# A weight stream in units of four blocks instead of eight, with five buffers for each split part instead of two

## The chip, the core and the metric

The kernel runs on one core of a Trainium2 chip. Its engines are TensorE (PE in the profile, with its weight loads as PEld), VectorE (DVE), ScalarE (ACT), GpSimd (POOL) and SyncE (SP, which issues nearly all the transfers here). The metric is the device time of one execution in microseconds (us); less is better.

## The reference

It is one step of a two-layer diffusion backbone over 128 context and 256 latent tokens, with 1024 features, in float32. Cut to what matters here:

```python
for l in range(2):                                   # per layer, for both streams of tokens
    mod = silu(c) @ w_ada[l] + b_ada[l]              # 9 modulations of 1024 features
    x = LN(alpha*x + 0.5*gate1 * ((silu(a)*g) @ ffn1_w_out))   # a, g = split(mod1(x) @ ffn1_w_in), 2816 wide
    z = mod2(x) @ w_in                               # inputs of the three mixers and of their gates
    o = sig(ga)*(window_attention(z) @ proj_a) + sig(gb)*(neighbourhood_attention(z) @ proj_b) \
        + sig(gc)*(rwkv_scans(z) @ proj_c)
    x = LN(alpha*x + gate2 * (o @ w_out))
    x = LN(alpha*x + 0.5*gate3 * swiglu2(mod3(x)))   # the second feed-forward, as the first
```

## The kernel before

All 384 tokens are one tile of 384 columns, and 128 features lie on the partitions, so a product of a weight block of 128x128 with 128 features of all tokens is one pass of PE with 384 columns. The weights (3344 blocks of 128x128 float32) come as one **stream** in the order of their use. Each block is split into two float32r parts: `hi`, a rounded copy that ACT writes, and `lo`, the rest, which DVE subtracts (`raw - hi`). With the activations split likewise, a block costs three matmuls: `wh xh`, `wh xl` and `wl xh` (`mm3`, lines 381 to 389, and `mm3_steps`, 391 to 401, which hands over two blocks at a time). Only the third one reads `lo`.

The class `Stream` does this in units. `fetch` (line 367) issues one transfer of a unit into a buffer `raw` on SP (line 369), one ACT instruction for `hi` and one or two DVE instructions for `lo`. All three tiles lie in rings: a transfer waits until the `lo` that read its buffer last is done, and an ACT copy waits until PE has used the last block of the unit that lay in its buffer of `hi` before.

Each engine runs its instructions in a fixed queue. A scheduler orders the queues ahead of the run by the program's order and by priorities: `tc.high_priority(offset=...)` around `fetch` lets a unit's instructions go ahead of the work around them by as much as the offset (1500 mostly, 100 beside the scans), as far as a buffer is free, and `tc.issue_after` ties an instruction behind another. Outside the steady state (`stream.steady` false, at the starts of phases) `stream.ahead()` places the units by hand.

The stages of a layer, with the names that the rows use:

- A **feed-forward** (`ffn`): products `pg` and `pa` of the first weight (lines 387 to 389), the gated result `si`, split into `uh` and `ul`, and products `po` of the second weight (lines 397 to 399). Beside the first feed-forward of layer 0, the second, and the first of layer 1, DVE also computes the modulations: `acc <- adaw, cs, acc`, 1024 columns each, whose weights `adaw` come in transfers of their own. In layer 0's first feed-forward the modulations that are needed at once are computed in a startup on PE (`ada`, line 1739).
- A layer norm (`Norm`) that goes with the last products: `ax` takes in `gate * po` chunk by chunk. After the fourth chunk a pilot mean `mu` is subtracted (`ax <- ax,mu`), and the sums go through `stat`, `sv`, `dd` and `rs`.
- A **head** (`Head`): the next phase's first products run already on an input without the norm's scale (`hd`, lines 699 to 701), and the scale is put in afterwards through `wb`, `si` and `sg` (before the mixers through `kx`, `vx`, `qx`).
- **Attention**, two kinds, among dense products `pz`; then the **RWKV scans**, with more dense products (`pz`, `pp`, `pc`) where the scans leave PE free; then the output projection (`po` again).

The names in front of the arrow are written, those behind it read; nearly all DVE, ACT and POOL instructions go through one helper and have its line, 290 (291 after the change).

Of the kernel before, what the change touches and what calls it, by code (L numbers as in the profile page):

```python
# [15 lines left out]
P = 128  # L16
# [13 lines left out]
UNIT = 8  # L30
# [161 lines left out]
# sets of four groups of 256 modulations; the first two are what the first chunks of features need, then the others  # L192
# [3 lines left out]
def _layout(inp):  # L196
    """Rearranges the inputs (permutations and concatenations only)."""
# [36 lines left out]
    # [l][d][h = (p, e)][v][k] -> [l][(e, k)][p][d][v]  # L234
# [8 lines left out]
def _weights(inp, order):  # L243
    """The large weights as 128 x 128 blocks in the order of their use."""
# [22 lines left out]
def _unlayout(r):  # L267
# [7 lines left out]
    st = r["o_st"].reshape(DEPTH, 2, HD, 4, 2, HD)  # l, e, k, p, d, v  # L275
# [4 lines left out]
class Engine:  # L280
    """An engine that knows its last instruction."""
# [14 lines left out]
def trunk(tc, I, O, order, taps=None, stop=None):  # L296
# [5 lines left out]
    def then(*engines):  # L302
        """Behind the last instruction so far of these engines."""
        st = ExitStack()
        for e in engines or (V, S, G):
            if e.last is not None:
                st.enter_context(tc.issue_after(e.last.ins))
        return st
# [32 lines left out]
    class Stream:  # L341
        def __init__(self):
            self.unit = 0
            self.left = []
            self.offset, self.parts, self.steady = 1500, 1, True
# [12 lines left out]
        def ahead(self):  # L358
            """Out of the steady state: the unit after the next is split as soon as the last is used up."""
            if len(self.left) <= UNIT and self.unit < WS_UNITS:  # L360
                self.fetch(self.offset)
# [4 lines left out]
        def fetch(self, offset=0):  # L366
            with tc.high_priority(offset=offset) if offset else ExitStack():
                raw = ring.tile([P, UNIT * P], F32, tag="raw", bufs=3, name="raw")
                nc.sync.dma_start(out=raw, in_=I["ws"][self.unit])
            self.unit += 1  # L370
            hi = ring.tile([P, UNIT * P], F32R, tag="hi", bufs=2, name="hi")
            lo = ring.tile([P, UNIT * P], F32R, tag="lo", bufs=2, name="lo")
            S.activation(out=hi, in_=raw, func=AF.Copy)
            n = UNIT * P // self.parts
            for j in range(0, UNIT * P, n):
                V.tensor_tensor(out=lo[:, j : j + n], in0=raw[:, j : j + n], in1=hi[:, j : j + n].bitcast(F32), op=ALU.subtract)
# [5 lines left out]
    def mm3(out, chunks, xs, after=()):  # L382
        """out += sum of W_k^T x_k, with both factors as sums of two float32r parts."""
# [7 lines left out]
    def mm3_steps(out, chunks, xs, step=2):  # L391
        """mm3 in steps of a few chunks, with what each costs."""
# [10 lines left out]
    def split(dst_h, dst_l, src, lo_eng):  # L403
        """src (SBUF or PSUM, float32) = dst_h + dst_l."""
# [30 lines left out]
    def ada_beside(pool, n):  # L435
        """The next n steps with the products on the vector engine: where that has time, and the tensor engine has not."""
# [38 lines left out]
    def ada_flush():  # L475
        """To columns: out[feature, (block, group, stream)]."""
# [20 lines left out]
    ax = [act.tile([P, NTOK], F32, name=f"ax{c}") for c in range(KD)]  # L497
    # (four more columns: see Norm)
# [8 lines left out]
    class Norm:  # L507
        """Layer norm over the features of y = alpha x + gate * out, chunk by chunk as out comes.
        The next phase's input is h = rs g1 (y - mu) + b1, g1 and b1 per feature and stream, rs and mu per token. Its
        first products W^T h run on z = g1 y, before rs and mu are known: rs W^T z - rs mu W^T g1 + W^T b1, with g1 and  # L510
        b1 as four more columns of z."""
# [1279 lines left out]
```

## Time and profile before

| | us |
|---|---|
| three runs | 2444.65, 2437.09, 2435.69 |
| their median | 2437.09 |
| the profiled execution's span | 2439.6 |

The profiled execution has no time of its own beside its span, which runs from its first to its last instruction; 2439.6 lies 2.5 us above the median of the runs and inside their spread. The stages on the profile's time, in us: startup to 42; layer 0's first feed-forward to 330, head and attention to 580, scans to 870, output projection to 932, second feed-forward to 1240; layer 1's first feed-forward to 1545, attention to 1785, scans to 2072, output projection to 2140, second feed-forward to the end.

How to read it: PE is the engine that is busy nearly all of the time, so the reader looks for the gaps in PE and for what ended each of them. "Waits" lists these by engine and line; a timeline shows what the releasing engine did instead; windows give the busy time of each engine in a stretch and the TensorE clock granted in it (1.00 is the upper level).

### The profile page before, as it was taken

To read this page: it belongs to the slowest core of one execution; us is meant where nothing else is said; L and a number is where in the kernel's file an instruction comes from. 1 tells how busy PE (TensorE), PEld (TensorE's weight loads), DVE (VectorE), ACT (ScalarE), POOL (GpSimd) and SP (SyncE) were. 2 spreads that over 40 slices of the span, in tenths; PEclk is the share of its full clock that TensorE was granted. 3 is DMA by queue.
4 is the path that set the end of the run, shared out by engine and by line. 5 is a ranking of instruction groups with operands and counts; after the bars stand their busy time and mean duration, and the time that the engine had idled before them with its cause. 6 is when DMAs were issued, how large, how long until landed. Compare 5 with 4: busy or idle time off the path is not lost.

```text
span 2439.6 us, 42863 instructions
## 1 busy us (share of the span) xinstructions
PE 2297.4 (94%) x17066; PEld 2106.5 (86%) x17066; DVE 1696.6 (70%) x2865; ACT 1056.4 (43%) x1942; POOL 550.0 (23%) x522
## 2 busy tenths in 40 slices
PE   7999999998899998999999999899989999999998
PEld 5999988897777788999889999889877777889997
DVE  3797886777767568786978954776787674665534
ACT  3333245655545445333243332555555454443332
POOL 2111422101122044211432113310022220542113
PEclk9999999999999999999999999999999999999999
DMA  8575644242111262665546743523321113534332
GB/s 314 193 240 198 191 122 130 84 111 78 40 57 47 72 209 95 191 217 180 180 147 205 244 130 122 154 81 91 112 70 39 51 50 90 204 102 140 130 121 87
DMA packets 125079, 324.54 MB, mean 133 GB/s; under 512 B 31568, under 2 KB 50256, under 8 KB 124880
## 3 DMA queue, kind: packets, MB, share of 16 engines
q1 hardware_dynamic: 124880, 321.81, 41.1%
q8 instruction: 134, 2.20, 0.4%
q14 instruction: 65, 0.53, 0.1%
HBM read 312.06 MB, written 9.70 MB: 132 GB/s over the span
## 4 chain that ended last, share of the span: by engine, by line
PE 71%; DVE 15%; ACT 5%; issue 4%; DMA 3%; POOL 2%; SPq 0%; POOLq 0%; ACTq 0%; DVEq 0%
PE po L399 5%; PE po L398 5%; PE po L397 5%; PE pa L387 4%; PE pg L389 4%; PE pa L388 4%; PE pg L387 4%; PE pg L388 4%; PE pa L389 4%; DVE lo L290 3%; DVE acc L290 2%; PE pz L397 2%; DMA adaw<-wada 2%; ACT hi L290 2%; PE pz L398 2%
## 5 line engine op out<-in xcount | busy, mean ns | idle before, releaser
L290 DVE TENSOR_TENSOR lo<-raw,hi 128x1024 fp32r<-128x1024 f32 (+1 forms) x472 | 583.8, 1246 | 305.9 <-ACT hi L290 303.8
L290 ACT ACTIVATE hi<-raw 128x1024 fp32r<-128x1024 f32 x418 | 441.7, 1058 | 785.0 <-issue 267.5
L290 DVE SCALAR_TENSOR_TENSOR acc<-adaw,cs,acc 128x1024 f32<-128x1024 f32 x224 | 292.3, 1327 | 0.0
L290 POOL TENSOR_TENSOR ul<-si,uh 128x384 fp32r<-128x384 f32 x88 | 126.3, 1435 | 579.3 <-ACT uh L290 579.3
L399 PE MATMUL po<-uh,lo 128*128 128x384 f32 x704 | 238.6, 339 | 6.3 <-DVE lo L290 6.3
L397 PE MATMUL po<-uh,hi 128*128 128x384 f32 x704 | 239.7, 340 | 0.0
L398 PE MATMUL po<-ul,hi 128*128 128x384 f32 x704 | 238.0, 338 | 0.0
L387 PE MATMUL pg<-zh,hi 128*128 128x384 f32 x656 | 224.1, 342 | 9.1 <-DVE si L290 9.1
L388 PE MATMUL pg<-zl,hi 128*128 128x384 f32 x656 | 223.8, 341 | 0.0
L389 PE MATMUL pg<-zh,lo 128*128 128x384 f32 x656 | 223.2, 340 | 0.0
L387 PE MATMUL pa<-zh,hi 128*128 128x384 f32 x632 | 216.2, 342 | 4.9 <-ACT si L290 4.4
L389 PE MATMUL pa<-zh,lo 128*128 128x384 f32 x632 | 213.8, 338 | 0.6 <-DVE lo L290 0.6
L388 PE MATMUL pa<-zl,hi 128*128 128x384 f32 x632 | 214.2, 339 | 0.0
L399 PEld LDWEIGHTS po<-uh,lo 128*128 128x128 f32 x704 | 133.5, 190 | 7.3 <-DVE lo L290 7.3
L397 PE MATMUL pz<-zh,hi 128*128 128x384 f32 x352 | 128.1, 364 | 8.5 <-ACT hi L290 5.7
L397 PEld LDWEIGHTS po<-uh,hi 128*128 128x128 f32 x704 | 133.7, 190 | 2.2 <-issue 0.8
L398 PEld LDWEIGHTS po<-ul,hi 128*128 128x128 f32 x704 | 133.5, 190 | 1.4 <-issue 0.8
L387 PEld LDWEIGHTS pg<-zh,hi 128*128 128x128 f32 x656 | 125.0, 191 | 10.0 <-ACT hi L290 6.7
L399 PE MATMUL pz<-zh,lo 128*128 128x384 f32 x352 | 126.3, 359 | 4.1 <-DVE lo L290 4.0
L387 PEld LDWEIGHTS pa<-zh,hi 128*128 128x128 f32 x632 | 119.1, 188 | 9.8 <-ACT si L290 5.3
L389 PEld LDWEIGHTS pg<-zh,lo 128*128 128x128 f32 x656 | 125.6, 191 | 1.6 <-issue 1.6
L388 PEld LDWEIGHTS pg<-zl,hi 128*128 128x128 f32 x656 | 125.0, 191 | 1.6 <-issue 1.6
(390 smaller groups left out, 5157.4 us busy)
## 6 DMA issues: line engine op xcount, KB each, us to landing
raw<-ws SPq DMA_DIRECT2D x418, 512.0 KB, 3.5
adaw<-wada SPq DMA_DIRECT2D x144, 512.0 KB, 4.8
bm<-rpb SPq DMA_DIRECT2D x64, 64.0 KB, 7.1
axd<-ax SPq DMA_DIRECT2D x16, 192.0 KB, 5.2
gcd<-gt SPq DMA_DIRECT2D x16, 192.0 KB, 4.7
gc<-gcd SPq DMA_DIRECT2D x16, 192.0 KB, 3.4
ax<-axd SPq DMA_DIRECT2D x16, 192.0 KB, 4.8
xt<-xt SPq DMA_DIRECT2D x8, 192.0 KB, 8.6
```

The costliest lines, as they stand in the source:

```text
L290: self.last = f(*a, **k)
L387: T.matmul(out, wh, xh, start=(k == 0), stop=False)
L388: T.matmul(out, wh, xl, start=False, stop=False)
L389: T.matmul(out, wl, xh, start=False, stop=(k == n - 1))
L397: T.matmul(out, wh, xh, start=(k == 0), stop=False)
L398: T.matmul(out, wh, xl, start=False, stop=False)
L399: T.matmul(out, wl, xh, start=False, stop=(k == n - 1))
```

## The change

A unit has 4 blocks (512 columns, 256 KB) instead of 8 (1024 columns, 512 KB). The ring of `raw` has 4 buffers instead of 3, those of `hi` and `lo` 5 instead of 2. In blocks, `raw` goes from 24 to 16 and each part from 16 to 20; the sum stays 56. `lo` is always written by one instruction a unit; before, it took two of 512 columns beside the scans and one of 1024 elsewhere. `ahead()` fetches units while 12 or fewer blocks are left, where it fetched one when 8 or fewer were left. The startup fetches four units ahead in place of two, the same 16 blocks. The rest of the difference is comments and line numbers.

```diff
-UNIT = 8
+UNIT = 4
+RAWS, PARTS = 4, 5
...
-            self.offset, self.parts, self.steady = 1500, 1, True
+            self.offset, self.steady = 1500, True
...
         def ahead(self):
-            if len(self.left) <= UNIT and self.unit < WS_UNITS:
+            while len(self.left) <= (PARTS - 2) * UNIT and self.unit < WS_UNITS:
                 self.fetch(self.offset)
...
         def fetch(self, offset=0):
             with tc.high_priority(offset=offset) if offset else ExitStack():
-                raw = ring.tile([P, UNIT * P], F32, tag="raw", bufs=3, name="raw")
+                raw = ring.tile([P, UNIT * P], F32, tag="raw", bufs=RAWS, name="raw")
                 nc.sync.dma_start(out=raw, in_=I["ws"][self.unit])
             self.unit += 1
-            hi = ring.tile([P, UNIT * P], F32R, tag="hi", bufs=2, name="hi")
-            lo = ring.tile([P, UNIT * P], F32R, tag="lo", bufs=2, name="lo")
+            hi = ring.tile([P, UNIT * P], F32R, tag="hi", bufs=PARTS, name="hi")
+            lo = ring.tile([P, UNIT * P], F32R, tag="lo", bufs=PARTS, name="lo")
             S.activation(out=hi, in_=raw, func=AF.Copy)
-            n = UNIT * P // self.parts
-            for j in range(0, UNIT * P, n):
-                V.tensor_tensor(out=lo[:, j : j + n], in0=raw[:, j : j + n], in1=hi[:, j : j + n].bitcast(F32), op=ALU.subtract)
+            V.tensor_tensor(out=lo, in0=raw, in1=hi.bitcast(F32), op=ALU.subtract)
...
-                stream.offset, stream.parts = 100, 2
+                stream.offset = 100
...
-                    for _ in range((2, 1, 0, 0)[c0 // 2]):
+                    for _ in range((4, 1, 0, 0)[c0 // 2]):
                         stream.fetch()
```

Over the whole queues, DVE has 364 instructions more, ACT 418 more and SP 418 more transfers; PE and POOL have as many as before. Three places of the queues:

The first is DVE in layer 0's first feed-forward, from the subtraction of the pilot mean on; before:

```order
L290 TENSOR_TENSOR ax_83<-ax_83,mu 128x384
L290 SCALAR_TENSOR_TENSOR acc<-adaw,cs,acc 128x1024
L290 TENSOR_TENSOR lo<-raw,hi 128x1024
L290 SCALAR_TENSOR_TENSOR acc<-adaw,cs,acc 128x1024 x3
L290 TENSOR_TENSOR lo<-raw,hi 128x1024
L290 SCALAR_TENSOR_TENSOR acc<-adaw,cs,acc 128x1024 x2
L290 TENSOR_TENSOR lo<-raw,hi 128x1024
L290 SCALAR_TENSOR_TENSOR ax_84<-po,gate,ax_84 128x128
```

and now:

```order
L291 TENSOR_TENSOR ax_83<-ax_83,mu 128x384
L291 SCALAR_TENSOR_TENSOR acc<-adaw,cs,acc 128x1024
L291 TENSOR_TENSOR lo<-raw,hi 128x512
L291 SCALAR_TENSOR_TENSOR acc<-adaw,cs,acc 128x1024
L291 TENSOR_TENSOR lo<-raw,hi 128x512
L291 SCALAR_TENSOR_TENSOR acc<-adaw,cs,acc 128x1024
L291 TENSOR_TENSOR lo<-raw,hi 128x512
L291 SCALAR_TENSOR_TENSOR acc<-adaw,cs,acc 128x1024
L291 TENSOR_TENSOR lo<-raw,hi 128x512
L291 SCALAR_TENSOR_TENSOR acc<-adaw,cs,acc 128x1024 x2
L291 TENSOR_TENSOR lo<-raw,hi 128x512
L291 SCALAR_TENSOR_TENSOR ax_84<-po,gate,ax_84 128x128
```

Two subtractions of 8 blocks stood between groups of one, three and two modulation products; five of 4 blocks stand now one behind each product, so that three products in a row are gone. What stands ahead of this place has also moved: 480 blocks are split there now, where it were 472.

The second is DVE at the start of a feed-forward, where the sums of the layer norm arrive (`sv`); before:

```order
L290 COPY sv<-stat 128x6
L290 TENSOR_TENSOR sv<-sv,stat 128x6
L290 TENSOR_TENSOR dd<-sv 128x3
L290 TENSOR_TENSOR lo<-raw,hi 128x1024
L290 TENSOR_TENSOR dd<-sv,dd 128x3
L290 TENSOR_TENSOR ax_79<-ax_79,mean 128x384
L290 TENSOR_TENSOR ax_80<-ax_80,mean 128x384
L290 RECIPROCAL rs<-dd 128x3
```

and now:

```order
L291 COPY sv<-stat 128x6
L291 SCALAR_TENSOR_TENSOR zl_100<-ax_85,gb,zh_99 128x256
L291 SCALAR_TENSOR_TENSOR zl_102<-ax_86,gb,zh_101 128x128
L291 SCALAR_TENSOR_TENSOR zl_102<-ax_86,gb,zh_101 128x256
L291 TENSOR_TENSOR lo<-raw,hi 128x512 x2
L291 TENSOR_TENSOR sv<-sv,stat 128x6
L291 TENSOR_TENSOR dd<-sv 128x3
L291 TENSOR_TENSOR dd<-sv,dd 128x3
L291 TENSOR_TENSOR ax_79<-ax_79,mean 128x384
L291 TENSOR_TENSOR ax_80<-ax_80,mean 128x384
L291 RECIPROCAL rs<-dd 128x3
```

The subtraction between the two `dd`, 8 blocks, has gone from there, and two of 4 blocks stand ahead of `sv <- sv,stat` instead. From there to the first `si`, DVE has 20 blocks to split where it had 32.

The third is ACT at the start of layer 1's mixers, behind the value input `vx`; before:

```order
L290 ACTIVATE vx<-vx,wb 128x128
L290 ACTIVATE vx<-vx,wb 128x256
L290 ACTIVATE zh_99<-h 128x384
L290 ACTIVATE zh_101<-h 128x384
L290 ACTIVATE hi<-raw 128x1024 x2
L290 ACT_TABLE_LOAD
L290 ACTIVATE ax_81<-pz 128x384
L290 ACTIVATE qx<-qx,wb 128x128
L290 ACTIVATE qx<-qx,wb 128x256
```

and now:

```order
L291 ACTIVATE vx<-vx,wb 128x128
L291 ACTIVATE vx<-vx,wb 128x256
L291 ACTIVATE zh_99<-h 128x384
L291 ACTIVATE zh_101<-h 128x384
L291 ACTIVATE hi<-raw 128x512 x5
L291 ACTIVATE qx<-qx,wb 128x128
L291 ACTIVATE hi<-raw 128x512
L291 ACTIVATE qx<-qx,wb 128x256
L291 ACTIVATE hi<-raw 128x512
L291 ACTIVATE vt<-vt 128x384
L291 ACT_TABLE_LOAD
L291 ACTIVATE ax_79<-ax_79,wb 128x128
```

The query input `qx` stood behind a table load and the copy `ax <- pz`; it now stands ahead of the table load, behind 20 blocks of `hi`, and another 8 blocks stand among its pieces.

## Rows read from the trace of the kernel before

**Rows 1.** The page, section 1: busy time of each engine over the span.

```profile
PE 2297.4 (94%) x17066; PEld 2106.5 (86%) x17066; DVE 1696.6 (70%) x2865; ACT 1056.4 (43%) x1942; POOL 550.0 (23%) x522
```

**Rows 2.** Windows: busy us of PE, PEld, DVE, ACT, POOL; PEclk; DMA share; GB/s.

```profile
50.00:100.00 50.00, 50.00 (x288) 50.00 (x287) 26.54 (x26) 17.57 (x24) 9.55 (x6) 1.00 0.53 175
100.00:150.00 50.00, 48.45 (x294) 45.73 (x293) 48.86 (x45) 16.50 (x24) 6.62 (x5) 1.00 0.77 251
320.00:332.00 12.00, 12.00 (x76) 11.24 (x75) 7.20 (x13) 4.38 (x9) 3.08 (x2) 1.00 0.35 103
1785.00:2072.00 287.00, 265.51 (x3447) 219.55 (x3446) 202.41 (x423) 143.60 (x267) 60.79 (x88) 0.98 0.19 58
303.80:306.70 2.90, 2.90 (x10) 2.90 (x10) 2.90 (x3) 0.00 (x0) 0.00 (x0) 0.50 0.64 181
```

**Rows 3.** Waits of PE: engine, line, what it waited for, total us, times, longest.

```profile
PE ada L1739 <- DMA adaw<-wada: 12.1, 11, 5.7
PE po L399 <- DVE lo L290: 9.5, 6, 3.2
PE pg L387 <- DVE si L290: 9.1, 3, 3.1
...
PE pz L397 <- ACT hi L290: 5.7, 6, 2.6
...
PE pa L387 <- ACT si L290: 4.4, 3, 1.5
PE pz L399 <- DVE lo L290: 4.0, 4, 1.1
...
PE hd L699 <- ACT hi L290: 2.7, 3, 0.9
```

**Rows 4.** Tile raw over the span: instructions that read or write it, min/median/max ns.

```profile
L290 DVE TENSOR_TENSOR lo<-raw,hi x472: 648/1225/2062, 16.1 to 2416.0; 128x1024 fp32r<-128x1024 f32 x122, 128x512 fp32r<-128x512 f32 x36
L369 SPq DMA_DIRECT2D raw<-ws x418: 327/328/913, 5.6 to 2404.8; - x140
L290 ACT ACTIVATE hi<-raw x418: 1038/1061/1069, 15.0 to 2414.9; 128x1024 fp32r<-128x1024 f32 x140
```

**Rows 5.** The tile's DMAs alone, from 60 to 230 us: issue to landing.

```profile
DMA to landing us min/median/max: 3.3/4.1/5.2
```

**Rows 6.** Groups by line and shape on DVE: busy us, mean ns, idle before.

```profile
L290 DVE TENSOR_TENSOR lo<-raw,hi 128x1024 fp32r<-128x1024 f32 x364 | 500.9, 1378 | 279.4 <-ACT hi L290 277.5 <-DMA gc<-gcd 0.7
...
L290 DVE TENSOR_TENSOR lo<-raw,hi 128x512 fp32r<-128x512 f32 x108 | 82.9, 802 | 26.5 <-ACT hi L290 26.3
```

**Rows 7.** The same view on ACT, the nearest operation of 512 columns.

```profile
L290 ACT ACTIVATE gt<-pb 128x512 f32<-128x512 f32 x16 | 9.5, 595 | 17.8 <-PE pb L1340 17.6
```

**Rows 8.** Timeline of DVE, 284 to 310 us: start, duration, instruction, idle before.

```profile
287.72 1.40 DVE L290 TENSOR_TENSOR lo<-raw,hi 128x1024 fp32r<-128x1024 f32 x1 [2.50 <-ACT hi L290]
...
295.63 5.75 DVE L290 SCALAR_TENSOR_TENSOR acc<-adaw,cs,acc 128x1024 f32<-128x1024 f32 x3
301.30 2.01 DVE L290 TENSOR_TENSOR lo<-raw,hi 128x1024 fp32r<-128x1024 f32 x1
```

**Rows 9.** Timeline of PE at the same place.

```profile
303.36 0.69 PE L399 MATMUL po<-uh,lo 128*128 128x384 f32 x1 [3.15 <-DVE lo L290]
```

**Rows 10.** Timeline of DVE, 1230 to 1284 us: the start of a feed-forward.

```profile
1240.57 0.16 DVE L290 TENSOR_TENSOR sv<-sv,stat 128x6 f32<-128x6 f32 x1 [3.17 <-PE stat L629]
...
1240.84 1.23 DVE L290 TENSOR_TENSOR lo<-raw,hi 128x1024 fp32r<-128x1024 f32 x1
...
1260.07 2.01 DVE L290 TENSOR_TENSOR lo<-raw,hi 128x1024 fp32r<-128x1024 f32 x1
...
1262.96 0.56 DVE L290 TENSOR_TENSOR si<-si,hrs 128x384 f32<-128x384 f32 x1
```

**Rows 11.** Timeline of PE at the same place.

```profile
1263.07 0.66 PE L387 MATMUL pg<-zh,hi 128*128 128x384 f32 x1 [2.96 <-DVE si L290]
```

**Rows 12.** DMA issues of 256 KB: line, count, KB each, median us to landing.

```profile
cvb<-cvb SPq DMA_DIRECT2D x2, 256.0 KB, 4.0
```

More of the change, by code (lines that the diff above doesn't have):

```diff
@@ L873, in mixer @@
                 add(1e9)
-                stream.offset, stream.parts = 1500, 1
+                stream.offset = 1500
             with tc.tile_pool(name=f"mo{l}", bufs=1) as pool:
```

## The prediction

> **What bounds the kernel now.** I read the page first: PE is busy 2297.4 of 2439.6 us [rows 1], so only 142.2 us are idle on it, and a change that leaves PE's instructions alone can win no more than that, plus what PE loses in matmuls at a lower clock. Then the windows. From 50 to 100 us, in a feed-forward without modulations, PE issues 288 matmuls in 50.00 us, one every 173.6 ns, with no gap [rows 2]: there the split is hidden whole, and finer units have nothing to win. From 100 to 150 us, beside the modulations, DVE is busy 48.86 of 50 [rows 2]; there the split competes for DVE. In a scan stage PE is busy 265.51 of 287 [rows 2], and most of those gaps end with results of the scans.
>
> The waits of PE [rows 3] then say which gaps belong to the weight stream. Directly: `po` on `lo` 9.5 us, `pz` on `hi` 5.7, `pz` on `lo` 4.0, `hd` on `hi` 2.7, with smaller ones some 26 us. Indirectly, because DVE or ACT was splitting while something urgent stood behind: `pg` on `si` 9.1 and `pa` on `si` 4.4. So about 40 us are in play, a third of which is long waits at five places.
>
> Two timelines show how these arise. At 295.63 us DVE runs three modulation products, 5.75 us, and only then, at 301.30, a `lo` of 8 blocks that takes 2.01 us [rows 8]; PE waits 3.15 us for it [rows 9]. [...] The other: at the start of a feed-forward a `lo` of 1.23 us stands between the two halves of the norm's statistics, and another of 2.01 us right before `wb` and `si` [rows 10], and PE waits 2.96 us for `si` [rows 11].
>
> **What the change costs.** It adds 364 DVE and 418 ACT instructions and 418 transfers. DVE takes 648 ns at the least for 512 columns, where the median, a whole unit, is 1225 [rows 4]: two for one cost 2x648-1225 = 71 ns. By the means, in which POOL's work on the same memory is mixed in, it is 2x802-1378 = 226 ns [rows 6]. I take 71 outside the scans, since the 802 is from the scan stages (where `lo` has that width already), and keep 226 as the bound: 26 to 82 us of DVE time in all. For ACT the nearest row of 512 columns is 595 ns [rows 7], against 1061 for a `hi` of 1024 [rows 4]: 2x595-1061 = 129 ns a unit, 54 us in all.
>
> [...]
>
> In a feed-forward without modulations DVE is busy 26.54 and ACT 17.57 of 50 us [rows 2], so nothing of this shows. Beside modulations twelve old units fall on 50 us: 48.86 + 12x0.071 = 49.7 at the low price, still under 50. In attention and scans DVE and ACT stand in the chains. The scans have 54 old units (108 pieces of `lo` [rows 6]); there DVE's pieces don't change, and ACT's 54x129 ns = 7 us lie partly on the path. I take +3 us for both layers' mixers, bounds 0 and +10.
>
> **What it gives.** *Pilot means* (in two of the three feed-forwards with modulations; the second wait is the 3.2 in [rows 3]). With one 4-block `lo` behind each product instead of 8 blocks behind three, and 480 instead of 472 blocks split at the pilot mean, the block that PE waited for at 303 us is split before the products begin. It can be split so early because 20 blocks have buffers instead of 16, and DVE stood idle 2.50 us just before, for want of a `hi` [rows 8]. Gain 2x(3.15+1.3) = 8.9 us. DVE has to give the time back somewhere: from 320 to 332 us it is busy 7.20 of 12 [rows 2], so 4.8 us of slack are left behind each pilot, just enough. Bounds 0 (if it is all waited for later) and -9.
>
> *Starts of feed-forwards* (three). The `lo` between the two `dd` goes into the 3.17 us that DVE waits for `stat` [rows 10], 1.1 us sooner for all that follows; 20 blocks instead of 32 from there to `si` take another 0.5 off it. The two smaller pieces right ahead of `si` hold the same 8 blocks as before, so of the 3 us wait [rows 3] about 1.5 stays. With half of the slow matmuls behind it: 3x(1.6+0.65) = 6.7 us. Bounds -4 and -13 (wait and slow matmuls gone).
>
> *Other direct waits.* PE needs the first blocks of a unit, and they come sooner: `hi` by 1061-595 = 0.47 us, `lo` by that and 1225-648 = 0.58 more. Three waits of `hd` lose 0.47 each, four of `pz` on `lo` (4.0) nearly all, the four small ones of `po` (9.5-3.15-3.2 = 3.2) most, those of `pz` on `hi` about 0.5 each for the two longest: up to 9 us. At the mixers' heads part is only moved to the next wait of the chain; I take -6, bounds -2 and -9.
>
> *Mixers' starts.* `qx` no longer stands behind the table load, but behind 20 blocks of `hi` and among 8 more. I take -2 for both layers, bounds +3 and -4.
>
> *Startup.* PE waits there for `adaw` [rows 3]; the stream's first units are as many bytes as before, in finer lots. -1, bounds 0 and -3.
>
> Sum: -8.9 -6.7 -6 -2 -1 +3 = -21.6, so 2418.0 against the profiled 2439.6. That span is 2.5 above the median of the runs; against the median it is 2415.5, and I predict 2416.
>
> **Rivals.** (a) *Larger gain*: the waits for `si` and the slow matmuls behind them go whole (-13 instead of -6.7), and the other terms reach their far bounds: 9+13+9+4+3-0 = 38 us at most, 2399 at the least; I place this case at 2396 to 2408. For it: DVE's queue is what stands before `si`, and each 1.1 us counts there. Against it: the same 8 blocks still stand right ahead of `si`.
>
> (b) *Moved, no change*: DVE stays the bound where it was, and the time comes back at the next result of DVE. At the pilots the slack is 4.8 us for 4.45 of gain and a dozen instructions more; if it fails there, 8.9 is lost, and with +10 in the mixers the sum is -21.6+8.9+7 = -6, about 2431. For it: 48.86 of 50 [rows 2].
>
> (c) *Slower, the split becomes the bound beside the modulations*: at 226 ns a unit, DVE needs 48.86+2.7 = 51.6 us in 50, so PE waits 1.6 us every 50 us of such a stretch; over some 550 us (my estimate: two thirds of three feed-forwards of 290 to 310 us) that is 17 us, and the pilots' gain (in the same stretches) is gone: -21.6+8.9+17+10 = +14, about 2452. It decides from a price of some 95 ns on, (50-48.86)/12, and turns the sum's sign near 200. Against it: POOL, whose work stretches `lo`, is busy 6.62 of 50 there [rows 2], so the low price is the nearer one.
>
> (d) *The `raw` ring starves*: it holds 16 blocks instead of 24. A transfer of 512 KB lands in 4.1 us beside the modulations, at most 5.2 [rows 5]; with 0.60 and 0.65 for the split a buffer is held 6.5 us, four of them give a unit every 1.6 us, and PE uses one in 12x173.6 ns = 2.08. It binds from a landing of 8.33-1.25 = 7.1 us. The one transfer of 256 KB in the trace took 4.0 [rows 12], so it should hold. If transfers queue behind each other on SP so that it fails in the same 550 us by a tenth, it is +55 us, 2470.
>
> [...]
>
> **How the numbers follow.** A difference of under 0.5% (12 us) can't be told from none in this kernel. The forecast case, 2408 to 2424, has 0.46; (a) 0.20; (b), 2425 to 2446, 0.22; (c) 0.09; (d) 0.03. Faster is the forecast and (a), with a little of (b) taken off for the border: 0.67; same 0.22; slower, from (c) and (d), 0.11. The range leaves out (c), (d) and the far ends of (a) and (b): 2398 to 2437.
>
> **What would show it.** Right: no wait of 3 us for `lo` near 300 and 1200 us, and granted clock 1.00 there; `pg` on `si` near 1.5 us three times; DVE's `lo` near 650 ns in the feed-forwards and ACT's `hi` near 600; the three feed-forwards with modulations shorter by some 4 to 7 us each; scans of equal length. Wrong: waits of `po` or `pg` for `lo` spread through 100 to 230 us (c), waits of ACT's `hi` for its transfer (d), longer scans, or a wait for a norm's statistics or `adam` that took the pilots' place (b).

## The result and the profile after

The changed kernel takes 2454.69 us, the median of 8 runs (2446.70 to 2469.71), and the kernel before 2438.18 (8 runs, 2433.42 to 2451.20). The ratio is 1.0069, with an interval of 1.0044 to 1.0093: slower by 0.7%, where I had forecast 0.9% faster, and outside my range. The profiled execution spans 2467.9 us and is the slowest of the eight; a second profile of the same kernel (run after_again) spans 2457.4. What stands in both belongs to the change, and what differs is scatter.

Section 1 of the page says first where the time went, in the first profile and in the second, to be held against [rows 1]:

```profile
PE 2324.7 (94%) x17066; PEld 2139.7 (87%) x17066; DVE 1729.3 (70%) x3229; ACT 1135.4 (46%) x2360; POOL 569.7 (23%) x522
```

```profile
PE 2316.9 (94%) x17066; PEld 2135.1 (87%) x17066; DVE 1732.8 (71%) x3229; ACT 1136.3 (46%) x2360; POOL 570.5 (23%) x522
```

PE's idle time, the span less the busy time, is 143.2 and 140.5 us, where it was 142.2: the waits that went and those that came balance. PE's busy time grew by 27.3 and 19.5 us with the same 17066 matmuls, the span by 28.3 and 17.8. Nearly all of this growth, 25 and 20 us, lies in the scan stages and output projections taken together. The granted clock fell with it: its mean over the span is 0.961 and 0.964, where it was 0.983. In the eight executions of the changed kernel it is 0.961 to 0.972, in those of the kernel before that ran beside the experiments 0.976 to 0.986. In the two traces PE's clock stands at the lower level, 0.50, for 193 and 176 us, in the one before for 81. So by the profile the same matmuls took longer, and the lower clock is what moved with it; a microsecond at the lower level has no fixed price, though (e5_all below has 142 of them and is busy as long as before).

The waits of PE in the profile after (engine, line, what it waited for, total us, times, longest) answer to [rows 3]:

```profile
PE ada L466 <- DVE acc L291: 18.4, 11, 5.8
PE pg L386 <- DVE si L291: 10.8, 3, 4.0
PE ada L1738 <- DMA adaw<-wada: 10.2, 8, 5.6
...
PE po L396 <- ACT mh L291: 7.1, 4, 1.9
...
PE sl L1038 <- DVE qs L291: 5.3, 2, 2.7
...
PE pz L396 <- ACT hi L291: 5.2, 2, 2.6
...
PE sc L1026 <- ACT qx L291: 3.8, 2, 2.3
...
PE pz L398 <- DVE lo L291: 1.5, 2, 0.8
PE po L396 <- ACT hi L291: 1.4, 2, 0.7
```

The waits for the weights' own parts shrank as forecast: `po` on `lo`, 9.5 us before, has left the list, and `pz` on `lo` fell from 4.0 to 1.5. `pa` on `si` (4.4 at the three starts of feed-forwards) is gone there too. New waits stand in their place: `ada` on `acc` rose from 6.9 us to 18.4 with a longest of 5.8, `mh` is at 7.1 where `po` waited 0.7 before, `qx` at 3.8 where it was 0.6, and `pg` on `si` rose from 9.1 to 10.8.

The groups of the page on the split instructions (busy us, mean ns) answer to [rows 4, 6]:

```profile
L291 ACT ACTIVATE hi<-raw 128x512 fp32r<-128x512 f32 x836 | 522.5, 630 | 864.9 <-PE po L397 230.4
L291 DVE TENSOR_TENSOR lo<-raw,hi 128x512 fp32r<-128x512 f32 x836 | 616.0, 743 | 386.2 <-ACT hi L291 378.7
L291 DVE SCALAR_TENSOR_TENSOR acc<-adaw,cs,acc 128x1024 f32<-128x1024 f32 x224 | 322.8, 1459 | 0.0
```

DVE spends 32 us more on `lo` than the 583.8 of before (500.9 and 82.9), ACT 81 us more on `hi` than 441.7, and the modulation products take 1459 ns each where they took 1327.

To see where the span went I cut both traces at the starts of the same instructions. Each figure is the distance of two such starts, in us; two figures are two layers, for "second weight" the two feed-forwards of layer 0.

| stretch | before | changed | second profile |
|---|---|---|---|
| first weight, layer 0: first `pg` to first `po` | 206.5 | 202.7 | 202.5 |
| second weight with pilot: first `po` to `sv` | 106.9, 106.9 | 108.4, 109.4 | 108.5, 108.5 |
| attention's start: first `sc` to first `sl` | 9.7, 8.4 | 14.1, 14.1 | 13.8, 13.9 |
| scan stage: first `up` to last `scan` | 283.7, 281.2 | 287.0, 285.2 | 278.4, 286.0 |
| output projection: last `scan` to `sv` | 71.3, 74.1 | 81.5, 81.4 | 80.9, 80.7 |

By the second profile the change gains 4 us in the first row and loses 3 in the second, 10 in the third and 16 in the last; the scans cancel (-5, +5), and about -7 of the rest leave the 17.8 us between 2439.6 and 2457.4. The third row of the kernel before scatters: b_single and b_mods (below) have the same queues there, and took 7.1 to 7.4 us.

**The pilots.** DVE and PE in the timelines after, at the place of [rows 8, 9]:

```profile
277.45 1.49 DVE L291 TENSOR_TENSOR lo<-raw,hi 128x512 fp32r<-128x512 f32 x1
278.87 2.03 DVE L291 SCALAR_TENSOR_TENSOR acc<-adaw,cs,acc 128x1024 f32<-128x1024 f32 x1
...
315.34 1.08 PE L466 MATMUL ada<-acc,conM 128*32 128x256 f32 x8 [5.75 <-DVE acc L291]
```

No matmul waits 3 us for `lo` any more. PE gets to the modulations' sums sooner, and they stand at the same place of its queue: behind 1521 dense matmuls (passes with a weight block) from the program's start, where it were 1522. There it waits 5.75 us for DVE's modulation products. DVE had no idle time to give: from 274 to 317 us it is busy 42.95 of 43.00. Behind the wait PE runs at the lower level, as the window (columns as in [rows 2]) shows:

```profile
315.30:318.70 3.40, 3.36 (x15) 2.30 (x15) 2.69 (x5) 0.63 (x1) 0.00 (x0) 0.50 0.49 143
```

In both profiles the lower level takes 6.8 us of each pilot's stretch, where it took 3.4 before.

**The output projection.** One chunk's way in the timelines after (DVE, POOL, ACT):

```profile
895.17 0.56 DVE L291 SCALAR_TENSOR_TENSOR ml<-ax,mh 128x384 fp32r<-128x384 f32 x1 [1.46 <-ACT mh L291]
895.65 0.55 DVE L291 SCALAR_TENSOR_TENSOR gc<-gc,pp 128x384 f32<-128x384 f32 x1
...
898.26 0.56 DVE L291 SCALAR_TENSOR_TENSOR ml<-ax,mh 128x384 fp32r<-128x384 f32 x1 [1.47 <-ACT mh L291]
...
896.28 1.40 POOL L291 TENSOR_TENSOR ax<-ax,gc 128x384 f32<-128x384 f32 x1 [1.69 <-DVE gc L291]
899.37 1.41 POOL L291 TENSOR_TENSOR ax<-ax,gc 128x384 f32<-128x384 f32 x1 [1.69 <-DVE gc L291]
...
897.71 0.53 ACT L291 ACTIVATE mh<-ax 128x384 fp32r<-128x384 f32 x1 [2.04 <-POOL ax L291]
```

It is a loop: `gc` on DVE, the sum on POOL, `mh` on ACT, `ml` on DVE, and only then the next `gc`, since DVE's queue is in order: 3.09 us a chunk. A projection of the merge takes four blocks. A unit of eight held two of them, and DVE's queue had two `gc`, one `lo` and two `ml`; in the trace before, POOL did the sums two by two, 4.68 us for two:

```profile
878.42 2.98 POOL L290 TENSOR_TENSOR ax<-ax,gc 128x384 f32<-128x384 f32 x2 [2.56 <-DVE gc L290]
883.10 2.98 POOL L290 TENSOR_TENSOR ax<-ax,gc 128x384 f32<-128x384 f32 x2 [1.70 <-DVE gc L290]
```

Besides, 147 dense matmuls stand between the last scan and the first product on `mh`, where there were 119; 29 fewer stand between the first scan and the last. At 173.6 ns [rows 2] the 28 are 4.9 us of PE's time a layer that only crossed the border between two rows of the table; but the scan stages did not get shorter by as much. In layer 0 the stretch up to the first product on `mh` grew by 4.6 us, with PE's busy time up by 4.8, and the one behind it by 5.1 to 5.6: there PE waits 3.2 to 3.5 us for `mh` and has the lower clock for 6.8 us, where it had none before.

**The attention's start.** ACT after, at the place of the third excerpt on the change:

```profile
1592.02 0.63 ACT L291 ACTIVATE hi<-raw 128x512 fp32r<-128x512 f32 x1 [5.84 <-DMA raw<-ws]
1592.56 0.39 ACT L291 ACTIVATE qx<-qx,wb 128x128 f32<-128x128 f32 x1
1592.85 0.61 ACT L291 ACTIVATE hi<-raw 128x512 fp32r<-128x512 f32 x1
1593.37 0.49 ACT L291 ACTIVATE qx<-qx,wb 128x256 f32<-128x256 f32 x1
```

The fifth `hi` ahead of `qx` waits 5.84 us for its transfer, and `qx`, whose input DVE had written by 1589.4, stands behind it. Over the whole trace ACT's `hi` waits 31.4 us for transfers, in 13 waits; before, 0.4.

**The scans** differ between the two profiles. In windows over one stretch (busy us of PE, PEld, DVE, ACT, POOL, then the granted clock), first the changed kernel, then its second profile:

```profile
684.00:708.00 24.00, 24.00 (x336) 18.40 (x337) 14.21 (x32) 10.35 (x20) 5.56 (x10) 0.51 0.19 52
```

```profile
684.00:708.00 24.00, 23.29 (x385) 19.01 (x385) 20.88 (x41) 13.67 (x26) 10.89 (x17) 0.93 0.22 65
```

The same queues ran for 24 us at the lower level in one execution (0.51 over the window) and for 3.4 in the other (0.93). The stage is 8.6 us shorter in the second, the larger part of the 10.5 us between the two profiles, and nothing that the change's order alone decides.

### The profile page after: what moved, and what is told of

The parts are those of the page before. It is cut to its first block, busy times and chain, and to the rows that moved or that the text cites. A ratio compares the mean times of both kernels' runs of the same rounds, so it can differ in the third digit from the quotient of the medians.

```text
span 2467.9 us, 45271 instructions
## 1 busy us (share of the span) xinstructions
PE 2324.7 (94%) x17066; PEld 2139.7 (87%) x17066; DVE 1729.3 (70%) x3229; ACT 1135.4 (46%) x2360; POOL 569.7 (23%) x522
## 5 line engine op out<-in xcount | busy, mean ns | idle before, releaser
L291 ACT ACTIVATE hi<-raw 128x512 fp32r<-128x512 f32 x836 | 522.5, 630 | 864.9 <-PE po L397 230.4
L291 DVE TENSOR_TENSOR lo<-raw,hi 128x512 fp32r<-128x512 f32 x836 | 616.0, 743 | 386.2 <-ACT hi L291 378.7
L291 DVE SCALAR_TENSOR_TENSOR acc<-adaw,cs,acc 128x1024 f32<-128x1024 f32 x224 | 322.8, 1459 | 0.0
L291 POOL TENSOR_TENSOR ul<-si,uh 128x384 fp32r<-128x384 f32 x88 | 148.4, 1687 | 551.4 <-ACT uh L291 551.4
L386 PE MATMUL pg<-zh,hi 128*128 128x384 f32 x656 | 225.2, 343 | 11.1 <-DVE si L291 10.8
L396 PE MATMUL pz<-zh,hi 128*128 128x384 f32 x352 | 136.7, 391 | 9.7 <-ACT hi L291 5.2
L397 PE MATMUL pz<-zl,hi 128*128 128x384 f32 x352 | 131.3, 373 | 1.3 <-POOL zl L291 1.3
```

The costliest lines, as they stand in the source:

```text
L291: self.last = f(*a, **k)
L386: T.matmul(out, wh, xh, start=(k == 0), stop=False)
L396: T.matmul(out, wh, xh, start=(k == 0), stop=False)
L397: T.matmul(out, wh, xl, start=False, stop=False)
```

## The experiments

Ratios are to the kernel before, run beside it on the same chip, with 95% intervals; its median there was 2439 to 2442 us.

**after_again**: the changed kernel once more.

> The changed kernel itself once more, for a second profile: the one shown, 2469.7 us, is the slowest of eight runs. All theories: about 2455 us. What repeats in both profiles belongs to the change, what differs is scatter of that execution: we expect the waits at the output projection (the merges 29.9 us long instead of 25.4), for acc at the pilots (5.8 us, twice) and for qx and qs at the attention's start to repeat to 0.2 us, and the clock in the scan stages to vary.

2461.33 us, 1.0093 (1.0059 to 1.0126). The waits repeat: `acc` 5.8 at the longest, `mh` 6.7 in all, `qx` 4.2, `qs` 5.3, those of `mh` and `qx` to 0.4 us and not to 0.2. The scan stages don't.

**e_44 and e_64**: the depths of the rings with units of four.

```diff
-RAWS, PARTS = 4, 5
+RAWS, PARTS = 4, 4      # e_44;  6, 4 in e_64
```

> RAWS, PARTS = 4, 4: units of four blocks, but parts no deeper than before (16 blocks), raw ring 16 blocks. Theory A (the order of the dense products beside the scans hangs on the depth of the parts): 453 instead of 429 dense matmuls stand again among the scans, the stretch from the scans' end to the output projection is back near 26 us from 29.9, and the kernel is 8 to 12 us faster than the changed one, some 2445. Rival B (the price of twice as many split instructions): the same time as the changed kernel, 2455. At the attention's start nothing changes by either, since the raw ring is the same: PE waits 1.5 to 2.3 us for qx.

> RAWS, PARTS = 6, 4: units of four blocks with the depths in blocks of the kernel before (raw 24, parts 16). Theory A, and that a raw ring of 16 blocks makes transfers late at the attention's start: against RAWS, PARTS = 4, 4 the waits of ACT's hi for its transfer (31 us in 13 waits in the changed kernel) go, PE's wait for qx falls under 0.5 us in both layers, and the time is another 4 to 6 us lower, about 2440. Rival: the transfers are not late because of the ring, but because other transfers stand before them on SP; then it is equal to 4, 4.

e_44: 2465.84 us, 1.0109 (1.0071 to 1.0146); e_64: 2478.66, 1.0165 (1.0127 to 1.0203). Theory A fell, in its time though not in its order. The 453 dense matmuls are back among the scans, and the output projection is 4 us shorter (77.0), but the scan stages are 296 us long; at the heads `hd` waits 9.7 us for `hi`. ACT's waits for transfers are 29.7 us in e_44 and 7.2 in e_64, as expected, and e_64 was no faster: `rope` waits 4.9 us for ACT twice instead. So the shallow `raw` ring does make transfers late, but a deeper one did not win the time back. What e_44 shows at the attention's start was expected by neither theory: in layer 1 the fifth `hi` waits 6.10 us for its transfer ahead of `qx` there too, but PE shows no wait for `qx`, and the start takes 8.5 and 8.4 us; in e_64, without that wait, it takes 13.8 and 13.4. Counted from `sv` to the first `sl`, the two layers take 50.9 and 50.5 us in e_44 and 52.9 and 52.5 in e_64, where it were 54.0 and 52.5 in the second profile and 49.3 and 48.1 before. So the late transfer alone does not set this stretch. Whether shallower parts by themselves cost time is not shown, since the intervals of e_44 and after_again overlap. Why e_64 is 13 us behind e_44 is open: the profiled executions differ by 1.1 us.

**e2_merge**: both `gc` of a pair ahead of both `ml`.

```diff
+                    if m % 2:
+                        for c in (m - 1, m):
+                            mh, ml = ms[c]
                             S.activation(out=mh, in_=ax[c], func=AF.Copy, scale=0.5)
+                            with then(V):
                                 V.scalar_tensor_tensor(out=ml, ...)
```

> The changed kernel with one edit in the output projection: mh and ml of two chunks are written behind both gc of the pair, which is the order that units of eight blocks gave. Theory C (units of four blocks bring one chunk each, so that DVE's queue makes a loop of gc, POOL's sum, ACT's mh and DVE's ml that takes 3.1 us a chunk, where pairs took 4.7 for two): the stretch from the last scan to the first product on mh goes from 29.9 to 25 or 26 us in both layers, waits for mh (3.5 us in each) go, and the kernel is 10 to 14 us faster than the changed one, about 2443. Rival: the stretch is longer for the 28 dense matmuls that were moved behind the scans (4.9 us); then it stays above 29 us.

2449.36 us, 1.0040 (1.0024 to 1.0055), 12 us below the changed kernel beside it (after_again), as expected; but the stretch from the last scan to `mh` went to 28.4 us, not to 25 or 26, and the whole projection to 79.1, 2 us less a layer. Nearly all of the 10.2 us between its profile and the second one of the changed kernel lies in the scans of layer 1 (274.7 against 286.0), which the edit doesn't touch: here total and mechanism don't agree, and the mechanism is better read from the next run.

**b_single**: the loop alone, in the kernel before. `ml_last` keeps the last `ml`.

```diff
-                    V.scalar_tensor_tensor(out=ml, ...)
+                    ml_last[0] = V.scalar_tensor_tensor(out=ml, ...)
...
+        with tc.issue_after(ml_last[0].ins) if name == "proj_c" and ml_last[0] is not None else ExitStack():
             V.scalar_tensor_tensor(out=th, in0=th, scalar=1.0, in1=pp[:, :NTOK], op0=ALU.add, op1=ALU.mult)
```

> The kernel before, units of eight blocks, with one edit in the output projection: each gc on DVE waits in the queue behind the ml of the chunk before, so that the chunks go one by one. The 119 dense matmuls behind the scans stay where they are. Theory C (the loop gc, POOL, mh, ml of 3.1 us a chunk): the stretch from the last scan to the first product on mh goes from 25.4 to 28 to 30 us in both layers and waits of po for mh appear as in the changed kernel; the kernel is 7 to 14 us slower than before, near 2450. Rival (the stretch was longer only for the 28 matmuls moved there): it stays near 25.4 and the time at 2440.

2453.79 us, 1.0059 (1.0036 to 1.0081). With units of eight and 119 matmuls where they were, forcing the chunks one by one lengthens the output projection to 79.6 and 78.4 us (71.3 and 74.1 before), and the waits for `mh` appear:

```profile
PE po L397 <- ACT mh L290: 5.6, 4, 1.9
```

So the loop by itself costs 12.5 us in the two layers, of the 16 that this stage lost. The moved matmuls do much the same by themselves (e2_merge has pairs and 147 matmuls, 79.1), and both together are little worse than either (81): the two don't add up, so the stretch seems to end with whichever chain is later. Run e6_all_rw80 below, with pairs and 128 matmuls, is back at 71.4.

**e3_mods, e7_mods8 and b_mods**: modulation products taken out of the pilots' stretch, in the changed kernel (e3_mods), in e5_all below (e7_mods8) and in the kernel before (b_mods).

```diff
-NF1 = ((32, 16), (32, 0))
-NF2 = ((24, 16), (8, 0))
+NF1 = ((36, 12), (32, 0))      # (40, 8) in e7_mods8
+NF2 = ((28, 12), (8, 0))      # (32, 8)
```

> The changed kernel with four of the sixteen modulation steps beside the second weight moved to the first part of the feed-forward (two feed-forwards; NF1 36, 12 and NF2 28, 12), eight DVE products of 1.3 to 2 us fewer behind the pilot mean. Theory D (the pilots' stall was not removed, it moved from lo to acc: DVE is the bound from the first product of the second weight to the modulations' sums): PE's two waits of 5.8 us for acc fall under 1.5, the stretches from the first po to the norm's sums go from 108.4 and 109.4 us to 103 to 105, and the kernel is 6 to 9 us faster than the changed one (2458, over both sets of its runs), about 2450. Rival: DVE is as full in the first part (49 of 50 us), so the work moved there makes PE wait for lo or acc there, and the time stays.

2449.31 us, 1.0037 (1.0015 to 1.0059). The two stretches fell to 104.8 and 105.1 us, and the longest wait for `acc` to 2.4, not under 1.5 as expected:

```profile
PE ada L466 <- DVE acc L291: 14.2, 15, 2.4
```

The first part paid 2.3 us of it in layer 0. DVE's load behind the pilot is what bounds the changed kernel there.

> The run e5_all with eight instead of four modulation steps moved (NF1 40, 8 and NF2 32, 8). Theory D goes on: the two waits of 2.4 us for acc behind the pilots go too, another 3 to 5 us, near 2427. Rival: DVE, at 49 of 50 us in the first part, cannot take more, and PE waits there for acc; then 2431 or more.

2431.69 us, 0.9959 (0.9941 to 0.9977), equal to e5_all, which it changes. Against e5_all the pilots' stretches fell from 104.8 and 105.0 us to 99.2 and 99.3, and the first parts of the feed-forwards grew by 5 and 7: the rival held, what is taken off DVE behind the pilot is paid ahead of it.

> The kernel before with the four modulation steps moved as in the run e3_mods. Theory D (DVE bounds the pilots' stretch, and PE's wait of 3.15 us for lo is only where it shows): PE's two waits of 3.2 us for lo shrink to under 1 and the stretches of 106.9 us get 2 to 4 us shorter; the kernel is 4 to 8 us faster than before, about 2434. Rival (the wait came of the unit's size, three products ahead of one lo of 8 blocks): the waits stay and the time too.

2441.69 us, 1.0007 (0.9993 to 1.0022): theory D failed for units of eight. Their waits for `lo` stay:

```profile
PE po L399 <- DVE lo L290: 10.5, 8, 3.0
```

In its queue a `lo` of 8 blocks still stands behind three products, and PE still waits 3.0 us for it; the stretches stay at 107.2 and 107.0. So the finer unit did remove a cause; the load then showed as the next.

**e4_ahd and b_ahd**: one hand-placed fetch less at the start of a phase.

```diff
-AHD = (4, 7)
+AHD = (4,)
```

> The changed kernel with one call of ahead() less at each start of a phase (AHD = (4,)), so that 8 blocks of hi instead of 20 stand on ACT between vx and qx. Theory E (five split instructions queued ahead of qx, the last of them waiting for a transfer that was issued late, hold up the attention's first scores): the stretch from the first context score to the first latent score goes from 14.0 us to 9 or 10 in both layers, PE's waits for qx (2.3 and 1.5) to under 0.7, and the kernel is 6 to 9 us faster than the changed one. Rival: the units left out there are missed by hd or pz right away; then waits of hd or pz for hi take the place and the time stays or grows.

2445.92 us, 1.0016 (0.9995 to 1.0036). The attention's start fell to 10.2 us in both layers and `qx` left the list of waits; `qs` fell from 5.3 to 1.0. The wait for a transfer did not vanish (4.22 us in layer 1): it moved ahead of `vx`, for which PE shows no wait; `rope` waits 2.0 us a layer for ACT's `vt`, where it waited 0.6. From `sv` to the first `sl` the layers take 47.4 and 49.0 us. So with 8 blocks of `hi` between `vx` and `qx` in place of 20 the time comes back, and theory E holds in that; by e_44 and e_64 the transfer's share in it stays open.

> The kernel before with AHD = (4,) alone. If this edit alone makes the kernel before some 8 us faster, as run b_mods_ahd (2433.8) against b_mods (2441.7) suggests, the finer units are worth 3 us at most beside it (e5_all, 2430.9). If it stays at 2441, that difference was scatter.

2431.95 us, 0.9961 (0.9946 to 0.9977): the same edit makes the kernel before faster by 0.4%. Its start of the attention takes 6.7 and 7.0 us, but the kernel before took 7.1 to 7.4 there in b_single and b_mods without this edit; from `sv` to the first `sl` it is 45.9 and 45.7 where these two had 47.0 to 48.2. Where the rest of the 8 us lies is not shown.

**e5_all, e6_all_rw80 and b_mods_ahd**: the edits together (merge, modulations, AHD); in e6 also the stream's offset beside the scans at 80 instead of 100; in b_mods_ahd the last two edits on the kernel before.

> The three edits together on the changed kernel: merges in pairs, four modulation steps moved, AHD = (4,). If theories C, D and E name separate waits, their gains add: 12 (measured) + 6 to 9 + 6 to 9, so some 2430 us, 8 below the kernel before. If DVE as a whole is what bounds (rival), each frees time that another takes, and it stays near 2445.

2430.90 us, 0.9960 (0.9947 to 0.9974): the gains add for the most part, and this beats both kernels. Its PE is idle for 130.8 us, 11 less than before, and busy for 2297.3, which is the 2297.4 of before: the longer busy time is gone.

> The same with the stream's offset beside the scans at 80 instead of 100, which puts 449 dense matmuls among the scans where 429 were (458 before). Theory F (the scans of the changed kernel run at the lower clock because the dense products beside them stand elsewhere): the time at granted clock 0.5 between the first up and the last scan, 23 to 51 us a layer in the changed kernel, comes down toward the 13 of before, and the scan stages are 3 to 6 us shorter each. Rival: the clock there follows single gaps that the order of dense work does not set; then no difference beyond scatter, 3 us.

2443.41 us, 1.0019 (0.9999 to 1.0039). The output projection came back to 71.4 us in both layers, 7 us less each, and the scan stages took more than that: 288 us instead of 279 and 276. The time at granted clock 0.5 in the scans is 31 us a layer, where e5_all has 34 and 24 and the changed kernel's profiles 31 to 55. Theory F fell: more dense work beside the scans doesn't keep the clock up by itself.

> The kernel before with both edits that need no units of four blocks: modulation steps moved and AHD = (4,). It says what the finer units themselves are worth beside run e5_all (2430.9). If they are worth nothing or less, this is at 2431 or below; if the three edits only pay with finer units, it is 5 us or more above. With units of eight blocks one call less leaves 8 blocks less split at the heads, so waits for hi may grow there (rival).

2433.83 us, 0.9971 (0.9955 to 0.9987), between the two values expected. Its interval and those of e5_all and b_ahd overlap: beside these edits, finer units are worth nothing that can be measured.

**b_halves**: the instruction counts alone.

```diff
-            S.activation(out=hi, in_=raw, func=AF.Copy)
             for j in range(0, UNIT * P, n):
+                S.activation(out=hi[:, j : j + n], in_=raw[:, j : j + n], func=AF.Copy)
```

with two pieces everywhere and everything else as before.

> The kernel before, transfers and rings of eight blocks, but hi and lo of every unit in two instructions of 512 columns: the instruction counts of the changed kernel without its units and buffers. Price theory (rival (c) of the prediction: instructions cost DVE and ACT time that PE waits for): the pilots' stretches (106.9 us) and the first parts of the feed-forwards with modulations (173 to 179 us) get longer by 1.5 us or more each, as 1.5 and 2 us of the changed kernel's pilots were, and the kernel is slower by 5 to 12 us. Theory of the grain (C, D, E): those stretches stay within 1 us, the merge stays near 25 us, and the time within 4 us of 2441, unless the scans are ordered otherwise.

2478.63 us, 1.0150 (1.0125 to 1.0174), but not where the price theory puts it. The pilots' stretches are 107.5 and 106.0 us, the first parts of the feed-forwards within 1 us of before: twice as many split instructions cost PE nothing there, with DVE busy for 1736.4 us in all, where the changed kernel has 1729.3. The loss is in the scan stages, 300 us each (283.7 and 281.2 before): 26 and 25 us more between the first `up` and the first `scan`, some of it won back behind. That stretch of layer 0, before and in b_halves:

```profile
577.60:661.20 83.60, 73.64 (x859) 60.58 (x858) 65.09 (x118) 43.09 (x82) 23.04 (x37) 0.96 0.16 49
```

```profile
583.20:692.70 109.50, 97.84 (x948) 81.86 (x947) 72.27 (x131) 49.27 (x100) 24.04 (x38) 0.81 0.15 47
```

The scheduler put 35 more dense matmuls there, 6 us at 173.6 ns; the granted clock is 0.81 where it was 0.96, which means 41 us at the lower level in place of 7; and `pb` waits 6.7 us for `bk` on POOL where it waited 1.6. Which of these began it is not shown, nor whether the order or the instructions' price set it off.

## Why the prediction was wrong

Most of the waits that the sum takes away did go. What failed is the slack that was to pay for the gain at the pilots, the term for the mixers' starts, the output projection, which the sum leaves at nothing, and the clock, which it counts on one side only.

*What bounds the kernel*: the waits were read rightly. I listed PE's waits for the weights' parts and what hung on them, and those did shrink. I did not ask which order of the queues had rested on units of eight, and new waits took as much as the old ones gave: PE's idle time is 140.5 to 143.2 us, where it was 142.2.

*The clock* stands in the sum only as something to be given back (1.3 us behind each pilot, half of the slow matmuls at the starts of feed-forwards). In the trace before, the 1.3 are nine matmuls that start 0.32 us apart, 0.15 more than the 173.6 ns [rows 2] at granted clock 1.00; at 0.50 they stand from 303.85 us on:

```profile
303.85 0.52 PE L397 MATMUL po<-uh,hi 128*128 128x384 f32 x1
304.17 0.52 PE L398 MATMUL po<-ul,hi 128*128 128x384 f32 x1
...
306.41 0.52 PE L399 MATMUL po<-uh,lo 128*128 128x384 f32 x1
306.73 0.38 PE L397 MATMUL po<-uh,hi 128*128 128x384 f32 x1
```

That the change gives the 1.3, or half of it, back was an estimate that no run shows: in the first profile the lower level takes 6.8 us behind each pilot, where it took 3.4, and 3.4, 6.8 and 6.8 at the starts of feed-forwards, where it took 3.4 each time. The sum has no term for time at the lower clock that the change might add: 81 us at that level became 193 and 176, and PE's busy time grew by 27.3 and 19.5 us, which is the whole loss. The sign that I had named, granted clock 1.00 at the pilots, did not come (0.50 from 315.30 to 318.70).

*The pilots* (-8.9 forecast, +1.5 to +2.5 each measured) is the step that I had named and mis-chosen: "4.8 us of slack are left behind each pilot, just enough". The slack lay behind the wait that decides. PE's next need, the sums of the modulations, comes at the same matmul of its queue as before, and DVE was full until then. This was rival (b); e3_mods shows it.

*The mixers' starts* (-2 forecast for both layers, bounds +3 and -4; +10 measured, and more against the 7.1 us of b_single and b_mods) had the wrong sign. I read from the queue that `qx` stood behind 20 blocks of `hi` and gave a figure without a sum. What I left out is that the last of them can't start before its transfer lands, and that a fixed queue hands this wait (5.84 and 6.68 us) on to all behind it. The ring of 16 blocks (rival (d)) makes the transfers late, as e_44 and e_64 show (29.7 us of such waits and 7.2); I had tested the ring for throughput (2.08 us a unit), where it holds, and not for a burst. e4_ahd shows that the blocks ahead of `qx` cost the time; that it is the transfer's wait and not the rest of that queue is argued from the trace, and e_44 speaks against it.

*The output projection* has no term in the sum. I counted its small waits for `lo` as a gain of 2 or 3 us, and did not look at its queue, where a unit's size had set how many chunks go round the loop together. It cost 16 us, the largest item; b_single shows what the loop alone costs (12.5), and some 10 of the 16 are the 28 dense matmuls a layer that came over from the scans.

*The starts of feed-forwards* (-6.7 forecast): from `sv` to the first `pg` on the new input -1.5, -1.5 and 0 us in the first profile, 0, -1.5 and 0 in the second. The wait of `pg` for `si` is no shorter (10.8 against 9.1, the longest 4.0). I had read one start [rows 10] for all three. In the other two a `lo` of 1.21 us stood right ahead of `si`, and two of 1.48 each stand there now: by the second profile `si` comes as late after `sv` as before, and PE is done with `hd` 0.9 us sooner and waits the longer. The wait of `pa` for `si` (4.4) did go.

*Startup and first part* (-1 forecast, at most -3): -4. *Other direct waits* (-6): `hd` on `hi` (2.7) is gone, `pz` on `lo` fell by 2.5 and the small ones of `po` on `lo` (3.2) went, while `pz` on `hi` stayed at 5.2 of 5.7; but at the heads and in the output projection the next link of the chain took their place.

*The price*: 202 ns a unit on ACT (2x630-1058) where I took 129, and on DVE 157 by the medians (2x691-1225, the 691 from the tile's own row after), where I had taken 71 from a shortest time. The trace before had it already: its 75 short `lo` during which POOL did nothing have a median of 684 ns, which makes 143; the 33 that ran beside a POOL instruction have 1214. After:

```profile
L291 DVE TENSOR_TENSOR lo<-raw,hi x836: 661/691/2768, 15.1 to 2441.9; 128x512 fp32r<-128x512 f32 x168
```

Rival (c) built on a high price, 226 ns a unit, and failed though the price was above my 71: b_halves has as many split instructions, and its feed-forwards are within 1 us of before.

*The scans* (+3 with the mixers): within their scatter, -5 to +5 a layer, though 4.9 us of dense work a layer had left them.

Open is why the scan stages of the changed kernel run 31 to 55 us a layer at the lower clock where before ran 10 to 14; about two thirds of all that the lower level gained lies there. Depth (e_44), the count of dense matmuls (e6_all_rw80) and split counts (b_halves) were tried and don't settle it.

## What to carry to other kernels

The size of a prefetch unit set here how work interleaves in the engines' fixed queues (two chunks of the output projection in 4.68 us before, one in 3.09 after). Before changing it, look for the places where one unit feeds a whole number of steps of a loop over several engines, and compare the queues there, not only where the weights are waited for. When a stall is to be removed, find the next thing that the same engine owes, at which instruction of the waiting engine it falls due, and whether there is slack before it, not behind it. An instruction that is moved ahead of an urgent one has to be costed with the transfer that it waits for. And hold PE's busy time against its idle time, with the granted clock beside them, before explaining a loss by waits alone: here the idle time stayed (142.2 us, then 143.2 and 140.5), and the matmuls took 27.3 and 19.5 us longer.

## What the runs showed of the hardware that was not expected

The modulation products on DVE, unchanged in shape and number, took 1459 ns on the mean instead of 1327. The traces say which: those during which POOL did nothing took 1273 ns on the mean before and 1272 after; those that ran beside a POOL instruction took 1459 before (65 of 224) and 1682 after (102). So the longer time goes with POOL's instructions beside them, and more products run beside one after the change; that the memory is the reason, as the prediction has it for `lo`, no run shows. POOL's `ul` took 1687 ns instead of 1435, but 1214 in b_halves, so it does not follow the number of split instructions. A transfer of 256 KB landed in 2.7 us at the median, one of 512 KB in 3.5 before; the one row of that size before, 4.0 [rows 12], was too high. And the same program's granted clock in one stretch of 24 us was 0.51 in one execution and 0.93 in another, with the stage 8.6 us longer in the first.
